# A two-layer decoder trunk on one core: transposing DMAs take a later place on SP's queue, and an unused two-column product goes ahead of the second layer's queries

## The chip, the core and the metric

The kernel runs on one core of one Trainium2 chip. A core has TensorE (PE: products, and PEld: its weight loads), VectorE (DVE), ScalarE (ACT), GpSimd (POOL) and SyncE (SP), each with a queue of its own that is worked off in order, and 16 DMA engines that all queues share. The metric is the time of the whole program on the device in microseconds. Engines wait for each other through semaphores only; an instruction that waits holds back all that stands behind it on its engine.

## What is computed

```python
DEPTH, SEQ, D_MODEL, D_FF = 2, 256, 1024, 2816
def reference(x, norm_mix, norm_ffn, hgrn_w_in, ..., ffn_w13, ffn_w2, final_norm):
    h = x                                          # (1, 256, 1024) float32
    for layer in range(DEPTH):
        y = rms_norm(h, norm_mix[layer])
        if layer % 2 == 0: y = hgrn2_mixer(y, ...)  # gated linear recurrence, 8 heads of 128
        else:              y = moba_mixer(y, ...)   # 8 heads of causal attention with a position bias
        h = h + y
        h = h + swiglu(rms_norm(h, norm_ffn[layer]), ffn_w13[layer], ffn_w2[layer])
    return rms_norm(h, final_norm)
def swiglu(h, w13, w2):
    g, u = jnp.split(h @ w13, 2, axis=-1)
    return (silu(g) * u) @ w2
```

With 256 tokens the second layer's attention is one causal block of 256 keys for each head; its queries, keys and values are `h @ w_in` in three parts of 1024 columns.

## The kernel before

**Products.** Each float32 operand is split into a high part and a rest (`xh`, `xl` of the activations, `whi`, `wlo` of the weights), and three products stand for one: `xh*whi`, `xh*wlo`, `xl*whi`. In most of the work (`mm_w`) a piece of 128 x 128 weights is loaded into TensorE and 256 tokens stream through it (products of 256 columns, out in features by tokens). Where the values, or the outputs of the second feed-forward matrix, are wanted in tokens by features (`mm_x`), 128 tokens are loaded and 512 columns of weights stream.

**Weights.** All weights lie in the order of their use in one tensor, in segments of 1024 columns x 128 rows. SP's queue loads a segment into a `raw` buffer (line 521; spare room in `ii` and `bt` serves as extra ones); ScalarE makes `whi` (line 497), VectorE `wlo` (line 502). Six pairs of `whi` and `wlo` exist, so the splits run at most six segments ahead of TensorE.

**Feed-forward.** Each layer has one. Its second matrix is applied by a scheme with 7 instead of 8 products (`Strassen`): it wants differences (`wdiff`, line 533, VectorE) and sums of weights (`wsum`, line 538, VectorE; another one by an accumulating DMA of GpSimd, line 546, that adds a segment onto a loaded one). The gate and up products are taken from PSUM by ScalarE (`gu`, line 1382) and worked into the hidden activations on VectorE and ScalarE (`sgq`, `uu`, `hx`).

**The residual, turned.** The residual `hT` lies in features by tokens; the feed-forward's results are added in tokens by features. So the residual is turned by DMA beside the first part of each feed-forward, in eight pieces of 128 features: ScalarE copies a piece into `flat` (one buffer; line 1505 in the first layer, 1702 in the second), a transposing DMA on SP's queue turns it into one of two `turns` buffers (lines 1508 and 1705), and ScalarE copies it to its place (lines 1511 and 1707). `Strassen.fold` reads it at the end of the feed-forward (line 1454).

**What sets the order.** Nothing is ordered by hand. TensorE's main products are written in the order of the code. All else goes through a planner (`Order`): `od.op(engine, cost, fn, reads, alloc, due, nbytes, late)` files an operation; while TensorE's clock of the plan moves on, `pump` puts on each engine's queue the filed operation that is due first among those that the plan holds ready. `ready` is the planned end of what an operation reads, and of the last use of the buffers it takes, plus 130 ns; a DMA's planned end is its issue, its bytes at 330 bytes a ns, 1900 ns and `late`. The plan only orders: what waits for what on the chip is set by semaphores. `LATE` is 2200 ns.

**Queries.** In the second layer `token_major` makes the values (512 columns each product, into `psA`), then `feature_major` makes for each head the queries and the keys: 24 products of 256 columns into one bank of PSUM. A bank holds 512 columns, of which these use 256. `Stats.finish` has a short product of two columns of its own, called `settle`, in the first layer (line 768).

Of the kernel before, what the change touches and what calls it, by code (L numbers as in the profile page):

```python
# [16 lines left out]
P = 128  # L17
S = 256
# [138 lines left out]


class Op:
    __slots__ = ("eng", "cost", "fn", "deps", "alloc", "due", "seq", "end", "nbytes", "early", "after", "late")  # L160


class Order:
# [15 lines left out]
        self.wait = {"V": [], "A": [], "G": [], "S": [], "T": []}  # L179
        self.seq = 0  # L180

    def op(self, eng, cost, fn, reads=(), writes=(), alloc=(), due=0.0, nbytes=0, early=None, late=0.0):
        o = Op()
        o.early = self.EARLY if early is None else early
        o.after, o.late = None, late
        o.eng, o.cost, o.fn, o.alloc, o.nbytes = eng, cost, fn, tuple(alloc), nbytes
        o.due, o.end, o.seq = self.tile + due, None, self.seq
        self.seq += 1
        deps = []
        for b in reads:  # L190
            deps += b.writers
        for b in writes:
            deps += b.readers
        o.deps = [d for d in dict.fromkeys(deps)]
        for b in reads:
            b.readers.append(o)
        for b in tuple(writes) + o.alloc:
            b.writers.append(o)
        self.wait[eng].append(o)
        return o  # L200
# [20 lines left out]
    def ready(self, o):  # L221
        if o.after is not None and o.after.end is None:
            return None
        t = 0.0
        for d in o.deps:
            if d.end is None:
                return None
            t = max(t, d.end)
        for b in o.alloc:
            f = self.free_at(b.ring)  # L230
            if f is None:
                return None
            t = max(t, f)
        return t + self.LAT

    def emit(self, o, t):
        start = max(t, self.now if o.eng == "T" else self.clock[o.eng])
# [87 lines left out]
def ca(n, ptr=0):  # L325
    return n / 1.2 + 93 + 93 * ptr
# [11 lines left out]
LATE = 2200.0  # L338
# [3 lines left out]
def hybrid_trunk(ctx: ExitStack, tc: tile.TileContext, wts, xT, par, gfin, tab, masks, out):  # L342
    nc = tc.nc
    V, A, G, T = nc.vector, nc.scalar, nc.gpsimd, nc.tensor
# [5 lines left out]
    od = Order()  # L350
# [57 lines left out]
    def bank(g, held=False):  # L408
        return rings["ps" + g].new(held)

    def main_bank(g):

        b = bank(g, held=True)
        r = b.ring
        od.need(lambda: od.free_at(r))
        b.tile = r.make()
        r.past.append(b)
        return b
# [7 lines left out]
    def wrote(b):  # L426
        b.writers = [Mark(od.now)]
# [8 lines left out]
    segs, c0 = [], 0  # L436
# [4 lines left out]
    quads, c = {}, 0  # L441
# [123 lines left out]
    def piece(name, layer, k, c0, n):  # L565
        assert plan[ws["piece"]] == (name, layer, k, c0, n), (plan[ws["piece"]], (name, layer, k, c0, n))
        ws["piece"] += 1
        return sub_piece("", n)
# [20 lines left out]
    def mm(o, a, b, start=False, stop=False):  # L589
        T.matmul(o, a, b, start=start, stop=stop, skip_group_check=True)  # L590
# [23 lines left out]
    def mm_w(o, w, x, start=False, stop=False):  # L614
        mm(o, w.hi, x.hi, start=start)
        od.main(MM)
        mm(o, w.lo, x.hi)
        od.main(MM)
        mm(o, w.hi, x.lo, stop=stop)
        od.main(MM, 1)  # L620
        od.pump()
# [52 lines left out]
    for k in range(KT):  # L674

        o = od.op("S", 60, lambda k=k: nc.sync.dma_start(hT[:, k:k + 1, :], xT[:, k:k + 1, :]),  # L676
                  writes=hb[k:k + 1], nbytes=131072, due=8 * k - 6)
        if k > 1:
# [12 lines left out]
    o = od.op("S", 60, lambda: nc.sync.dma_start(mk.tile, masks), writes=[mk], nbytes=NMK * P, due=65)  # L691
# [6 lines left out]
          due=100).deps.append(Issued(13))  # L698
# [178 lines left out]
            keep["from"] = None  # L877
            free_subs(ws["sub"])

    def feature_major(name, layer, c0, x, g):  # L880
        b = main_bank(g)
        for k in range(KT):
            mm_w(b[:, :S], piece(name, layer, k, c0, P), x[k], start=(k == 0), stop=(k == KT - 1))
        wrote(b)
        b.held = False
        return b
# [6 lines left out]
    for i in range(4):  # L893
# [6 lines left out]
          reads=[pv, x0[3].l], writes=[lbm], due=50)  # L900
    for i in range(2):
        od.op("V", 80, lambda i=i: V.tensor_tensor(le[:, i], gain(5 + i), lbm.tile, op=OP.subtract), reads=[lbm],
              writes=[le], due=50)
# [5 lines left out]
          writes=[oml], due=60)  # L909
# [251 lines left out]
    for h in range(NH):  # L1161
        c = Core(h)
        xx = xs if h else x0
        c.forget(feature_major("hgrn_w_in", 0, D + P * h, xx, "B"))
        c.query(feature_major("hgrn_w_in", 0, P * h, xx, "B"))
        c.gate(feature_major("hgrn_w_in", 0, 3 * D + P * h, xx, "B"))
        c.result()
        for b in (*c.Q.values(), *c.K.values(), c.even, c.k1, c.kk):
            old.readers += b.readers + b.writers
        if h == 0:  # L1170
            for k in range(KT):
                x0[k].free()
# [68 lines left out]
    class Place:  # L1241


        end = None
# [19 lines left out]
    c = 0  # L1264
# [225 lines left out]
    x2 = {k: X("x", k) for k in range(KT)}  # L1490
# [12 lines left out]
    def flip_h0(k):  # L1503
        a, b, due = flat.new(), rings["turns"].new(), 60 + 24 * k
        od.op("A", ca(2 * S), lambda: A.activation(a.tile.rearrange("p (z t) -> p z t", z=2),
                                                   words(hT[:, k, :]).rearrange("p (t z) -> p z t", z=2), AF.Copy),
              reads=hb[k:k + 1], alloc=[a], due=due)
        od.op("S", 1200, lambda: nc.sync.dma_start(b.tile.rearrange("p (c f) -> p c f", c=4), a.tile, transpose=True),
              reads=[a], alloc=[b], nbytes=131072, due=due, late=LATE)
        for tt in range(2):  # L1510
            od.op("A", ca(S), lambda tt=tt: A.activation(
                words(halves0[tt][:, k * P:k * P + P]).rearrange("p (f z) -> p f z", z=2),
                b.tile.rearrange("p (z a f) -> p a f z", z=2, a=2)[:, tt], AF.Copy), reads=[b], due=due + 12,
                writes=[quadrants[tt, k // 4][0]])

    for k in range(KT):
        flip_h0(k)
    f = Strassen(0, x1, st1, "A", {"A": (1, 5, 4), "B": (6, 3, 7, 2)}, quadrants,
                 {(1, 0): 7, (0, 0): 9, (0, 1): 11, (1, 1): 13})
# [34 lines left out]
    for nh, tt in ((0, 1), (0, 0), (1, 0), (1, 1)):  # L1554
        b = f.final[nh, tt]
# [5 lines left out]
        if (nh, tt) == (0, 0):  # L1561
# [4 lines left out]
            due=0).deps.extend(f.folds[tt, nh])  # L1566
# [107 lines left out]
              reads=[b3, hi], alloc=[lo], due=22)  # L1674

    for h in range(NH):
        qb = feature_major("moba_w_in", 0, P * h, x2, "A")
        kb = feature_major("moba_w_in", 0, D + P * h, x2, "A")
        attend(h, qb, kb)
    for k in range(KT):  # L1680
# [18 lines left out]
    def flip_h(k):  # L1699

        a, b, due = flat.new(), rings["turns"].new(), 60 + 24 * k
        od.op("A", ca(2 * S), lambda: A.activation(a.tile.rearrange("p (z t) -> p z t", z=2),
                                                   words(hT[:, k, :]).rearrange("p (t z) -> p z t", z=2), AF.Copy),
              reads=hb[k:k + 1], alloc=[a], due=due)
        od.op("S", 60, lambda: nc.sync.dma_start(b.tile.rearrange("p (c f) -> p c f", c=4), a.tile, transpose=True),
              reads=[a], alloc=[b], nbytes=131072, due=due)
        o = od.op("A", ca(2 * S), lambda: A.activation(
            words(ht[:, :, k * P:k * P + P]).rearrange("p a (f z) -> p a f z", z=2),
            b.tile.rearrange("p (z a f) -> p a f z", z=2, a=2), AF.Copy), reads=[b], due=due + 12,
            **(dict(writes=[ht]) if k else dict(alloc=[ht])))  # L1710
        if k:
            o.deps.append(ht.writers[0])

    for k in range(KT):
        flip_h(k)
# [4 lines left out]
    class Final:  # L1720
# [38 lines left out]
        def end(self):  # L1759
# [6 lines left out]
            roots.append(od.op("A", 100, lambda: A.activation(a.tile, s[:, e:e + 1], AF.Sqrt, bias=w[:, :1]), reads=[s, w],  # L1766
                               alloc=[a], due=due))
            one = (lambda o, x, y, op: V.tensor_tensor(o, x, y, op=op)) if tt else \
                (lambda o, x, y, op: V.tensor_scalar(o, x, y, None, op0=op))
            od.op("V", 80, lambda: one(w[:, 1:2], s[:, e:e + 1], w[:, :1], OP.add), reads=[s, w], writes=[w], due=due)  # L1770
# [13 lines left out]
            for i, (lo, n) in enumerate(((192, 320), (0, 192), (512, 256), (768, 256)) if tt else ((0, 512), (512, 512))):  # L1784
# [19 lines left out]
                else:  # L1804
# [3 lines left out]
    f = Strassen(1, x3, st3, "B", {"A": (1, 2, 5, 3), "B": (4, 6, 7)}, quadrants,  # L1808
                 {(0, 1): 15, 2: 18, (0, 0): 20, (1, 0): 25, (1, 1): 28}, lambda: od.op(
        "A", ca(D), lambda: A.activation(gf.tile, gf.tile, AF.Copy, scale=2 * float(D) ** 0.5), reads=[bt], writes=[gf],  # L1810
        due=30))
# [4 lines left out]
    for tt in range(2):  # L1816
        fin = Final(tt)
        for i, (nh, o, n) in enumerate(FIN[tt]):
            b = final[nh, tt]
            f.wait_fold(nh, tt)  # L1820
            for k in f.ks:
                p = w[k, nh]
# [46 lines left out]
```

## Time and profile before

| | |
|---|---|
| time, median of 3 runs | 596.44 us (596.27 to 597.47) |
| the profiled execution | 595.67 us; span of its instructions 593.9 us |
| granted TensorE clock | 0.999 |
| busy: TensorE, VectorE, ScalarE, GpSimd | 585.8, 512.9, 444.2, 59.7 us |
| transposing DMAs, first layer (line 1508) | 8, issued 139.5 to 203.8 us |
| transposing DMAs, second layer (line 1705) | 8, issued 413.7 to 457.7 us |
| values of the second layer end, queries begin | 336.96 us |
| SP's issue of one transposing DMA (second layer) | 1.2 us, landing 2.4 to 5.5 us later (median 3.0) |

All times of rows are microseconds from the first instruction. Rows of a timeline give start, length, engine, line, operation, out<-in, and in brackets the idle time of that engine just before, with what ended it. The lengths of TensorE's products overlap (a product of 256 columns is shown as 0.28 us and the next starts some 0.11 us later), so its pace is read from starts. "PEld" waits are waits of its weight loads. Where a row is merged (x51), its second number is the time that all of them take.

### The profile page before, as it was taken

How to read it: one execution, taken by the hardware profiler on the slowest of the kernel's cores; microseconds unless marked ns; L12 is line 12 of the kernel's file. 1: busy time of each engine (PE TensorE's matmuls, PEld its weight loads, DVE VectorE, ACT ScalarE, POOL GpSimd, SP SyncE). 2: the span in 40 equal slices, each digit the busy share in tenths (PEclk: the TensorE clock that was granted, in tenths of full speed). 3: DMA queues.
4: the chain of work that ended last, by engine and by line, in shares of the span. 5: the costliest groups of instructions: out<-in, count | busy, mean ns of one | idle time of the engine just before them, and what ended most of it. 6: DMA issues, size and time to landing. Idle time of an engine off the chain costs nothing.

```text
span 593.9 us, 11985 instructions
## 1 busy us (share of the span) xinstructions
PE 585.8 (99%) x4439; PEld 557.0 (94%) x4439; DVE 512.9 (86%) x939; ACT 444.2 (75%) x868; POOL 59.7 (10%) x111
## 2 busy tenths in 40 slices
PE   9999999999999999999999999999999999999995
PEld 7899999999999999999988899999999999999984
DVE  5899988869897989999999688877798888888996
ACT  6898998957787767667749778976897766666763
POOL 0044131501100000000000000001100000000003
PEclk9999999999999999999999999999999999999999
DMA  8955552557678898877658877767778977877712
GB/s 279 368 165 196 178 171 85 171 178 208 173 228 225 220 249 255 260 241 236 211 196 219 245 253 192 233 162 242 196 200 233 302 243 239 229 231 225 210 35 73
DMA packets 58755, 125.53 MB, mean 211 GB/s; under 512 B 24712, under 2 KB 29704, under 8 KB 58696
## 3 DMA queue, kind: packets, MB, share of 16 engines
q1 hardware_dynamic: 55352, 115.31, 60.4%
q0 software_dynamic: 2384, 8.72, 8.8%
q10 hardware_dynamic: 960, 0.72, 0.4%
q8 instruction: 35, 0.57, 0.4%
q14 instruction: 24, 0.20, 0.1%
HBM read 118.64 MB, written 1.38 MB: 202 GB/s over the span
## 4 chain that ended last, share of the span: by engine, by line
PE 98%; DMA 1%; DVE 0%; ACT 0%; SPq 0%; issue 0%; DVEq 0%; ACTq 0%
PE psB L590 51%; PE psA L590 47%; DMA raw<-in_w_dram 1%; DVE raw L1791 0%; DVE raw L1737 0%; PE psB L1532 0%; PE psA L765 0%; ACT whi L490 0%; SPq L521 0%; SPq L676 0%; DVEq L1865 0%; ACT fa L1766 0%; ACT sq L1740 0%; DVE fw L1774 0%; PE psB L765 0%
## 5 line engine op out<-in xcount | busy, mean ns | idle before, releaser
L502 DVE TENSOR_TENSOR wlo<-raw,whi 128x1024 fp32r<-128x1024 f32 (+2 forms) x187 | 220.5, 1196 | 22.7 <-ACT whi L497 21.0
L497 ACT ACTIVATE whi<-raw 128x1024 fp32r<-128x1024 f32 (+1 forms) x185 | 188.0, 1035 | 20.2 <-PE psB L590 6.0
L590 PE MATMUL psB<-xh,whi 128*128 128x256 f32 x602 | 169.4, 285 | 0.0
L590 PE MATMUL psB<-xh,wlo 128*128 128x256 f32 x602 | 164.6, 277 | 0.0
L590 PE MATMUL psB<-xl,whi 128*128 128x256 f32 x602 | 160.0, 277 | 0.0
L590 PE MATMUL psA<-xh,whi 128*128 128x256 f32 x539 | 147.4, 277 | 0.0
L590 PE MATMUL psA<-xh,wlo 128*128 128x256 f32 x539 | 147.1, 277 | 0.0
L590 PE MATMUL psA<-xl,whi 128*128 128x256 f32 x539 | 142.3, 277 | 0.0
L590 PEld LDWEIGHTS psB<-xh,wlo 128*128 128x128 f32 x602 | 113.3, 188 | 0.6
L590 PEld LDWEIGHTS psB<-xh,whi 128*128 128x128 f32 x602 | 113.3, 188 | 0.5
L590 PEld LDWEIGHTS psB<-xl,whi 128*128 128x128 f32 x602 | 110.1, 188 | 0.0
L590 PEld LDWEIGHTS psA<-xh,wlo 128*128 128x128 f32 x539 | 101.3, 188 | 0.5
L590 PEld LDWEIGHTS psA<-xh,whi 128*128 128x128 f32 x539 | 101.2, 188 | 0.6
L590 PEld LDWEIGHTS psA<-xl,whi 128*128 128x128 f32 x539 | 98.2, 188 | 0.0
L590 PE MATMUL psB<-whi,hx 128*128 128x512 f32 x174 | 60.0, 392 | 0.0
L590 PE MATMUL psA<-whi,hx 128*128 128x512 f32 (+1 forms) x150 | 51.9, 379 | 0.0
L590 PEld LDWEIGHTS psB<-whi,hx 128*128 128x128 f32 x174 | 32.6, 188 | 6.4
L1386 ACT ACTIVATE sgq<-sgq 128x256 f32<-128x256 f32 x44 | 18.1, 414 | 24.1 <-DVE sgq L1384 24.0
L590 PE MATMUL psB<-wlo,hx 128*128 128x512 f32 x87 | 34.2, 393 | 0.0
L590 PEld LDWEIGHTS psA<-whi,hx 128*128 128x128 f32 x150 | 27.7, 188 | 4.3
L546 POOL DMA_DIRECT2D raw<-in_w_dram x13 | 11.3, 872 | 198.3 <-DVE wsum L538 158.9
L590 PE MATMUL psA<-wlo,hx 128*128 128x512 f32 (+1 forms) x75 | 28.6, 381 | 0.0
(263 smaller groups left out, 947.8 us busy)
## 6 DMA issues: line engine op xcount, KB each, us to landing
raw<-in_w_dram SPq DMA_DIRECT2D x176, 512.0 KB, 4.5
bt<-in_w_dram SPq DMA_DIRECT2D x15, 512.0 KB, 4.8
raw<-in_w_dram POOLq DMA_DIRECT2D x13, 512.0 KB, 5.7
ii<-in_w_dram SPq DMA_DIRECT2D x9, 512.0 KB, 4.3
raw<-in_w_dram SPq DMA_DIRECT2D x7, 256.0 KB, 5.6
hT<-in_x_dram SPq DMA_DIRECT2D x8, 128.0 KB, 5.4
bt<-scr SPq DMA_DIRECT2D x32, 32.0 KB, 5.3
bt<-in_w_dram POOLq DMA_DIRECT2D x2, 512.0 KB, 7.1
```

Of the source, the lines that this page charges most:

```text
L497: oa = od.op("A", ca(n), lambda h=h, r=src, o=o, n=n: A.activation(h[:, :n], r[:, o:o + n], AF.Copy), reads=[src], alloc=[h], due=due)
L502: V.tensor_tensor(lo[:, c:c + m], r[:, o + c:o + c + m], h[:, c:c + m].bitcast(FT), op=OP.subtract)
L546: od.op("G", 1000, lambda: nc.gpsimd.dma_start(b.tile, wts[c0 // CHUNK], accum_op=OP.add), writes=[b], nbytes=2 * 524288, due=due + 1)
L590: T.matmul(o, a, b, start=start, stop=stop, skip_group_check=True)
L1386: od.op("A", ca(S), lambda: A.activation(s.tile, s.tile, AF.Silu), reads=[s], writes=[s], due=due)
```

## The change

1. `Order.op` gets a `lag` that is added to the planned readiness of an operation, and the transposing DMAs of both layers get 3000 ns of it: the plan takes one up 3 us later than it holds its input finished.
2. In the second layer they are also given the planned cost and `late` that those of the first have (1200 ns instead of 60, and `LATE`).
3. `feature_major` of the first head's queries starts with a product of 128 x 128 activations with two columns of themselves into two unused columns of its bank. Nothing reads it.

```diff
-    def op(self, eng, cost, fn, reads=(), writes=(), alloc=(), due=0.0, nbytes=0, early=None, late=0.0):
+    def op(self, eng, cost, fn, reads=(), writes=(), alloc=(), due=0.0, nbytes=0, early=None, late=0.0, lag=0.0):
...
-        o.after, o.late = None, late
+        o.after, o.late, o.lag = None, late, lag
...
-        return t + self.LAT
+        return t + self.LAT + o.lag
...
-    def feature_major(name, layer, c0, x, g):
+    def feature_major(name, layer, c0, x, g, settle=False):
         b = main_bank(g)
+        if settle:
+            mm(b[:, S:S + 2], x[0].hi[:, :P], x[0].hi[:, :2], start=True, stop=True)
...
         od.op("S", 1200, lambda: nc.sync.dma_start(b.tile.rearrange("p (c f) -> p c f", c=4), a.tile, transpose=True),
-              reads=[a], alloc=[b], nbytes=131072, due=due, late=LATE)
+              reads=[a], alloc=[b], nbytes=131072, due=due, late=LATE, lag=3000.0)
...
-        qb = feature_major("moba_w_in", 0, P * h, x2, "A")
+        qb = feature_major("moba_w_in", 0, P * h, x2, "A", settle=(h == 0))
...
-        od.op("S", 60, lambda: nc.sync.dma_start(b.tile.rearrange("p (c f) -> p c f", c=4), a.tile, transpose=True),
-              reads=[a], alloc=[b], nbytes=131072, due=due)
+        od.op("S", 1200, lambda: nc.sync.dma_start(b.tile.rearrange("p (c f) -> p c f", c=4), a.tile, transpose=True),
+              reads=[a], alloc=[b], nbytes=131072, due=due, late=LATE, lag=3000.0)
```

The order of instructions differs at these places. First TensorE, between the last of the values and the first of the queries; before:

```order
L590 MATMUL psA<-whi,xh_4443 128x512
L590 MATMUL psA<-wlo,xh_4443 128x512
L590 MATMUL psA<-whi,xl_4452 128x512
L590 MATMUL psA<-xh_4293,whi 128x256
L590 MATMUL psA<-xh_4293,wlo 128x256
L590 MATMUL psA<-xl_4301,whi 128x256
```

and now:

```order
L590 MATMUL psA<-whi,xh_4443 128x512
L590 MATMUL psA<-wlo,xh_4443 128x512
L590 MATMUL psA<-whi,xl_4452 128x512
L590 MATMUL psA<-xh_4293 128x2
L590 MATMUL psA<-xh_4293,whi 128x256
L590 MATMUL psA<-xh_4293,wlo 128x256
L590 MATMUL psA<-xl_4301,whi 128x256
```

TensorE's queue has the one product more, and is otherwise the same from end to end.

SP's queue in the first layer's feed-forward, where the seventh and the eighth transposing DMA stood (`bt<-scr` are small loads of a table); before:

```order
L521 DMA raw_88<-in_w_dram 128x1024
L1508 DMA_TRANSPOSE turns_2147<-flat 128x4x128
L521 DMA raw_91<-in_w_dram 128x1024
L1277 DMA bt<-scr 16x4x128
L521 DMA raw_86<-in_w_dram 128x1024
L521 DMA ii<-in_w_dram 128x1024
L1277 DMA bt<-scr 16x4x128
L521 DMA raw_89<-in_w_dram 128x1024
L1508 DMA_TRANSPOSE turns_2148<-flat 128x4x128
```

and now, with the fifth and the sixth (lines below the first change are two higher):

```order
L521 DMA raw_90<-in_w_dram 128x1024
L1510 DMA_TRANSPOSE turns_2147<-flat 128x4x128
L521 DMA raw_87<-in_w_dram 128x1024
L1279 DMA bt<-scr 16x4x128
L521 DMA raw_88<-in_w_dram 128x1024
L521 DMA raw_91<-in_w_dram 128x1024
L1279 DMA bt<-scr 16x4x128
L521 DMA raw_86<-in_w_dram 128x1024
L521 DMA ii<-in_w_dram 128x1024
L1279 DMA bt<-scr 16x4x128
L1510 DMA_TRANSPOSE turns_2148<-flat 128x4x128
```

The loads keep their order among themselves; the first transpose has as many loads ahead of it in both layers' new places or more, the eighth of the first layer nine more and the eighth of the second 18 more.

VectorE in the same feed-forward, behind the split of a sum of weights; before:

```order
L502 TENSOR_TENSOR wlo<-wsum,whi 128x1024
L502 TENSOR_TENSOR wlo<-raw_90,whi 128x1024
L502 TENSOR_TENSOR wlo<-raw_91,whi 128x1024
L1384 TENSOR_TENSOR sgq<-gu,rrow 128x256
L533 TENSOR_TENSOR wdiff<-raw_86 128x512
L538 TENSOR_TENSOR wsum<-raw_86,ii 128x1024
L1392 TENSOR_TENSOR uu<-gu,sgq 128x256
L502 TENSOR_TENSOR wlo<-wdiff,whi 128x512
```

and now:

```order
L502 TENSOR_TENSOR wlo<-wsum,whi 128x1024
L533 TENSOR_TENSOR wdiff<-raw_86 128x512
L538 TENSOR_TENSOR wsum<-raw_86,ii 128x1024
L502 TENSOR_TENSOR wlo<-raw_90,whi 128x1024
L1386 TENSOR_TENSOR sgq<-gu,rrow 128x256
L502 TENSOR_TENSOR wlo<-raw_91,whi 128x1024
L1394 TENSOR_TENSOR uu<-gu,sgq 128x256
L502 TENSOR_TENSOR wlo<-wdiff,whi 128x512
```

The difference and the sum of the next weights now stand ahead of two splits. ScalarE's copies around the transposes move with them, and small swaps of the same kind stand at some other places of VectorE and ScalarE in both feed-forwards; every engine has the same instructions as before but for the one product.

More of the change, by code (lines that the diff above doesn't have):

```diff
@@ L159 @@
 class Op:
-    __slots__ = ("eng", "cost", "fn", "deps", "alloc", "due", "seq", "end", "nbytes", "early", "after", "late")
+    __slots__ = ("eng", "cost", "fn", "deps", "alloc", "due", "seq", "end", "nbytes", "early", "after", "late", "lag")
 class Order:
```

## The prediction

> **What bounds the kernel now.** I read the page first (busy times, the chain that ended last), then the stretches, then TensorE's own waits, then TensorE's and the queues' rows in time at the two places where the change can touch it.
>
> The page, busy time of each engine and the chain that ended last:
>
> ```profile
> PE 585.8 (99%) x4439; PEld 557.0 (94%) x4439; DVE 512.9 (86%) x939; ACT 444.2 (75%) x868; POOL 59.7 (10%) x111
> ...
> PE 98%; DMA 1%; DVE 0%; ACT 0%; SPq 0%; issue 0%; DVEq 0%; ACTq 0%
> ```
>
> The end of the run is set by TensorE's stream of products almost alone. The stretches say where (columns: stretch, its length, busy of TensorE, of its weight loads, VectorE, ScalarE, GpSimd with counts, granted clock, DMA share, GB/s):
>
> ```profile
> 139.50:336.90 197.40, 197.40 (x1397) 183.26 (x1397) 176.53 (x274) 143.45 (x235) 11.00 (x12) 1.00 0.78 226
> 336.90:347.90 11.00, 11.00 (x94) 10.96 (x94) 8.64 (x14) 7.39 (x11) 0.00 (x0) 1.00 1.02 336
> 347.90:587.00 239.10, 239.09 (x1874) 229.67 (x1872) 206.90 (x374) 176.37 (x303) 12.92 (x15) 1.00 0.69 203
> ```
>
> From 139.5 us on, which is the part of the order that the change rewrites, TensorE is busy in all but 0.01 us, at the full clock. Rows overlap, so a busy TensorE may still be slowed; its waits are therefore looked at on the weight loads, here all of them from 139.5 to 336.9 us (us in total, times, longest):
>
> ```profile
> PEld psB L590 <- DVE wlo L502: 0.2, 1, 0.2
> PEld psA L590 <- DVE wlo L502: 0.2, 1, 0.2
> PEld psA L590 <- DVE xl L706: 0.2, 1, 0.2
> ```
>
> From 336.9 us to the last product there is no such wait. So what an earlier arrival of anything can win behind 139.5 us is at most these 0.6 us, plus whatever makes the products themselves come faster.
>
> **The change, part by part.**
>
> *The two-column product.* It stands between the last product of the values (512 columns) and the first of the queries (256 columns). TensorE's rows at both ends of the stretch it opens, the group of one of its three operand kinds (31 of each), and a piece of the chain right behind it:
>
> ```profile
> 336.73 0.39 PE L590 MATMUL psA<-whi,xl 128*128 128x512 f32 x1
> 336.96 0.28 PE L590 MATMUL psA<-xh,whi 128*128 128x256 f32 x1
> ...
> 347.91 0.38 PE L590 MATMUL psB<-ff,sgf 128*128 128x128 f32 x2
> ...
> L590 PE MATMUL psA<-xl,whi 128*128 128x256 f32 x31 | 8.7, 281 | 0.0
> ...
> 348.65 5.78 PE psA L590 x51
> ```
>
> From 336.96 to 347.91 us 3 x 31 = 93 products start: 10.95 / 93 = 117.7 ns each. Behind the first scores, the same kind of product on the same operands comes every 5.78 / 51 = 113.3 ns. There are two paces, and the stretch of the change runs in the slower one for its whole length, with no engine waited for. If the short product puts TensorE in the faster pace, 4.4 ns are won on each product.
>
> What the short product itself costs is shown by the one that layer 1 has already, at 134.79 us, and its followers:
>
> ```profile
> 134.79 0.25 PE L590 MATMUL psA<-xh 128*128 128x2 f32 x1
> 134.91 0.36 PE L590 MATMUL psB<-xh,whi 128*128 128x256 f32 x1
> 135.11 0.28 PE L590 MATMUL psB<-xh,wlo 128*128 128x256 f32 x1
> 135.22 0.28 PE L590 MATMUL psB<-xl,whi 128*128 128x256 f32 x1
> 135.35 0.28 PE L590 MATMUL psB<-xh,whi 128*128 128x256 f32 x1
> 135.46 0.28 PE L590 MATMUL psB<-xh,wlo 128*128 128x256 f32 x1
> ...
> 53.67 1.77 PE psB L590 x15
> ```
>
> The short product and the four behind it take 135.46 - 134.79 = 0.67 us, where four at the fast pace are 0.45: a cost of 0.22 us. So the stretch becomes 0.67 + 89 x 0.1133 = 10.75 us instead of 10.95: **-0.20 us**. Bounds: if it cost nothing, 93 x 4.4 ns = -0.41; if the slow pace stays, +0.22. The last row above is why the second is possible: right behind products of 128 columns, 15 products at 53.67 us ran at 1.77 / 15 = 118 ns, so an interruption does not always end the slow pace. I take the middle because the only two-column product in the trace was followed by 113 ns.
>
> The Trainium skill (TensorE: Matmul & The Clock Gate, "Wait — 56ns, not 53.3ns?") gives one start-to-start time for a warm stream, N / 2.4 GHz plus about 2.5 ns, and a floor of about 25 ns for the smallest product. By it 256 columns come every 109 ns (an estimate from that page), there is no slow pace to leave, and the short product is pure cost: 0.03 - 0.16 = -0.13 us, 596.3 us by that page. The trace disagrees on the pace, since the same form shows both 117.7 and 113.3 ns, and on the floor, since the product behind the short one starts 0.12 us after it and the next 0.20 later.
>
> *The transposing DMAs of layer 1* (eight, line 1508). Seven of them move back on SP's queue, by one weight load (the first) to nine (the last), and the ScalarE copies that feed and empty them (0.6 and 2 x 0.4 us) move with it. Nothing is added. On SP a moved one delays what stands behind it by its issue, 1.2 us, as before. What it can free is a wait of SP, and one such wait can be followed to TensorE. SP's rows, the sum of its waits at line 1508 behind one ScalarE line, GpSimd's accumulating load and the landing times of all of its kind (min/median/max), then ScalarE, VectorE and TensorE:
>
> ```profile
> 189.67 0.38 SPq L521 DMA_DIRECT2D raw<-in_w_dram  x1
> 195.91 1.20 SPq L1508 DMA_TRANSPOSE turns<-flat  x1
> 197.22 0.52 SPq L521 DMA_DIRECT2D raw<-in_w_dram  x1
> 198.30 0.38 SPq L521 DMA_DIRECT2D raw<-in_w_dram  x1
> ...
> SPq L1508 <- ACT gu L1382: 8.8, 2, 6.4
> ...
> 200.51 0.86 POOL L546 DMA_DIRECT2D raw<-in_w_dram  x1 [16.96 <-DVE wsum L538]
> ...
> DMA to landing us min/median/max: 5.3/5.9/8.8
> ...
> 209.38 1.06 ACT L497 ACTIVATE whi<-raw 128x1024 fp32r<-128x1024 f32 x1 [2.14 <-DMA raw<-in_w_dram]
> ...
> 210.47 1.23 DVE L502 TENSOR_TENSOR wlo<-raw,whi 128x1024 fp32r<-128x1024 f32 x1 [2.48 <-ACT whi L497]
> ...
> 211.48 0.39 PE L590 MATMUL psA<-whi,hx 128*128 128x512 f32 x1
> 211.76 0.51 PE L590 MATMUL psA<-wlo,hx 128*128 128x512 f32 x1
> 212.10 0.40 PE L590 MATMUL psA<-whi,hx 128*128 128x512 f32 x1
> ```
>
> SP stands at the seventh transpose from 190.1 to 195.9 us because ScalarE has not made its input. The loads it held back then start in a burst, the accumulating load joins them at 200.51 and lands at its longest, 8.8 us later; ScalarE waits 2.14 us for it, VectorE 2.48, and TensorE's two products from 211.48 to 212.10 us take 0.28 and 0.34 us where one of 512 columns takes 336.96 - 336.73 = 0.23. That is 0.16 us of delay. In the new order the fifth transpose stands some two loads ahead of this place and the sixth behind it: inputs that are older than the seventh's here, so SP should stand less and the loads come evenly. Bounds: nothing freed, 0; all freed, -0.16. I take **-0.16**, since landing at the median would have brought the data 2.9 us earlier and 0.2 are enough.
>
> *VectorE's order behind it.* The same rewrite puts a difference and a sum (`wdiff`, `wsum`) ahead of one split of weights. VectorE there, and the product that reads the split first:
>
> ```profile
> 222.68 0.42 DVE L1392 TENSOR_TENSOR uu<-gu,sgq 128x256 f32<-128x256 f32 x1 [0.48 <-ACT sgq L1386]
> ...
> 226.56 1.22 DVE L502 TENSOR_TENSOR wlo<-wsum,whi 128x1024 fp32r<-128x1024 f32 x1
> 227.69 2.35 DVE L502 TENSOR_TENSOR wlo<-raw,whi 128x1024 fp32r<-128x1024 f32 x2
> ...
> 230.30 0.69 DVE L533 TENSOR_TENSOR wdiff<-raw 128x512 f32<-128x512 f32 x1
> 230.90 1.22 DVE L538 TENSOR_TENSOR wsum<-raw,ii 128x1024 f32<-128x1024 f32 x1
> ...
> 230.36 0.28 PE L590 MATMUL psA<-xh,wlo 128*128 128x256 f32 x1
> ```
>
> The first of the two splits ends at 227.69 + 1.22 = 228.91 us, 1.45 us ahead of its product. The two operations that now come first take 0.60 + 1.14 us (start to start), 1.74: late by 0.29. That happens if VectorE reaches this place as late as before. Between 210.47 us and here its longest idle time is the 0.48 us of the first row, so the 2.48 us lost above are what mostly set its lateness; with them gone the split is in time. So the two terms exclude each other: 0 here when the first is won (taken), **+0.29** when it is not.
>
> *The transposing DMAs of layer 2* (eight, line 1705), and where their result is first read:
>
> ```profile
> L1705 SPq DMA_TRANSPOSE turns<-flat x8: 1195/1197/1688, 413.7 to 457.7; - x8
> ...
> 574.69 0.75 DVE L1454 SCALAR_TENSOR_TENSOR ii<-psA,ny,ii 128x512 f32<-128x512 f32 x1 [0.32 <-PE psA L590]
> ```
>
> The last one moves back by 18 weight loads on SP's queue. At 2.7 us a load it is issued near 506 us (an estimate: 457.7 + 18 x 2.7, from 24 products of 113.3 ns for each load of 1024 columns), 68 us ahead of its reader. No TensorE wait exists in this part, so nothing is there to win: 0. If the cover went, a ScalarE pass of 0.7 us late in a split would show first.
>
> Sum: -0.20 - 0.16 + 0 + 0 = **-0.36 us**. It is made against the profiled execution, 595.67 us (span 593.9 and 1.77 around it), so 595.3 there. The median of the runs is 596.44, 0.77 above it; the forecast is 596.44 - 0.36 = **596.1 us**.
>
> **The rivals.**
>
> *SP's burst stays.* The transpose that now stands between the loads still meets the accumulating load on the DMA queues. For it: the number of transfers is the same. Then -0.20 and +0.29: 596.5 us.
>
> *The short product doesn't do what it is there for.* TensorE keeps the 117.7 ns: +0.22 - 0.16 = +0.06, 596.5 us. For it speaks the row of 53.67 us, against it that of 134.79. The Trainium skill's single pace (the page named above) would have the same effect.
>
> *The short product costs next to nothing*: -0.41 - 0.16, 595.9 us. Against it: 0.20 us between the products behind the one in layer 1.
>
> *Slower.* VectorE's difference at the second place now stands ahead of a split and waits for its own load; in the old order it had until 230.30 us. If that load lands late, the split behind it is late with it, and TensorE stops. For the whole to reach +1.2 us against the -0.20 of the short product, TensorE must stop for 1.4: the difference then starts at 227.69 + 1.4 - 0.29 = 228.8 us or later, 1.1 us after VectorE gets there. A load that is 2 us late (the worst accumulating load is 2.9 above its median) gives 0.29 + 2.0 - 0.20 = +2.1: 598.5 us. Against it: in the old order the difference ran without any wait.
>
> *Faster by much.* Not from these parts: -0.41 and the whole 0.6 us of waits make 1.0 us, under the 1.2 below.
>
> **How the numbers follow.** A difference of 0.2%, 1.2 us, is about what a measurement of this kernel can tell from none; the three runs alone lie between 596.27 and 597.47. Forecast 0.45; burst stays 0.22; short product without effect 0.15; short product free 0.05: all of these, 0.87, lie within 0.2%. Slower 0.08. Faster 0.05, for something that this trace does not show. The range takes the four middle cases, 595.9 to 596.5, and the scatter of a median of few runs, half a microsecond: 595.4 to 597.0.
>
> **What would show it.** Right: TensorE's products from the query stretch to the first scores at 113.3 ns each (some 10.75 us in all), no wait of weight loads near 211 us, SP at line 1510 with far less waiting than at 1508. Wrong: 117.7 ns behind the short product; a stop of TensorE near 230 us behind line 502; or any wait of TensorE behind 347 us, where there is none now. A time under 595 or over 598 would say that the bound was not TensorE's stream as I read it.

## The result and the profile after

The changed kernel takes 600.04 us (median of 15 runs, 597.13 to 602.37) against 596.44 (15 runs, 594.84 to 599.33): slower by 0.53%, ratio 1.0053 with a 95% interval of 1.0039 to 1.0067, some 3.2 us by the ratio and 3.6 between the medians. The profiled execution took 597.44 us (span 595.7), near the short end of its runs, so it shows less than the usual loss. Busy time of TensorE and the shares of the chain that ended last, on the page after:

```profile
PE 586.9 (99%) x4440; PEld 557.2 (94%) x4440; DVE 513.2 (86%) x939; ACT 444.2 (75%) x868; POOL 60.9 (10%) x111
...
PE 78%; DMA 8%; DVE 6%; ACT 4%; issue 2%; POOL 1%; SPq 1%; DVEq 0%; ACTq 0%
```

TensorE is as busy as before to 0.2%, and yet only 78% of the chain runs through it, where it was 98%: the chain now leaves it for weight loads, their splits and their sums. The waits of weight loads from 190 us on (us in total, times, longest):

```profile
PEld psB L590 <- ACT gu L1384: 1.0, 1, 1.0
PEld psA L590 <- ACT gu L1384: 0.9, 1, 0.9
PEld psB L590 <- DVE wlo L502: 0.6, 1, 0.6
PEld psA L590 <- DVE xl L706: 0.2, 1, 0.2
```

The last one stood in the kernel before as well. The two on `psB` are in the second layer's feed-forward, where the kernel before had none. The place in rows of TensorE, after:

```profile
517.97 0.39 PE L590 MATMUL psB<-whi,hx 128*128 128x512 f32 x1
518.52 0.51 PE L590 MATMUL psB<-wlo,hx 128*128 128x512 f32 x1 [0.16 <-DVE wlo L502]
...
519.56 0.39 PE L590 MATMUL psB<-whi,hx 128*128 128x512 f32 x1
520.49 0.39 PE L590 MATMUL psB<-xh,whi 128*128 128x256 f32 x1 [0.54 <-ACT gu L1384]
```

Two products of 512 columns take 0.55 and 0.93 us where 0.23 is usual: 1.0 us lost, and 0.1 more on the product behind each. Product by product, TensorE is 0.99 us later than in the kernel before at 516.59 us (515.60 there) and 2.25 at 520.71 (518.46 there), and this difference stays to the end. So 1.25 us are lost here and nothing else behind the queries; of the 1 us ahead of it, some 0.4 lies in the first layer's feed-forward, 0.1 at the short product, and some 0.4 in the first 140 us, which the change doesn't touch. What the two products wait for begins at an accumulating load of GpSimd. That load, the split that waits for it and what is queued behind it on ScalarE, after:

```profile
506.12 0.86 POOL L546 DMA_DIRECT2D raw<-in_w_dram  x1 [15.06 <-DVE wsum L538]
...
514.13 1.06 ACT L497 ACTIVATE whi<-raw 128x1024 fp32r<-128x1024 f32 x1 [2.26 <-DMA raw<-in_w_dram]
...
516.86 0.68 ACT L1709 ACTIVATE ii<-turns 128x512 uint16<-128x512 uint16 x1
...
519.34 0.62 ACT L497 ACTIVATE whi<-wdiff 128x512 fp32r<-128x512 f32 x1
519.86 0.58 ACT L1384 ACTIVATE gu<-psB 128x512 f32<-128x512 f32 x1
```

ScalarE stands 2.26 us for the load, and the copy `gu`, which empties the bank that TensorE wants next, comes behind all of it, with a copy out of `turns` (0.68 us) and the split of `wdiff` (0.62 us) among it; before, the copy stood elsewhere and that split behind `gu`. The low part of the same sum of weights on VectorE and the first product that reads it, before (the first fence) and after (the second):

```profile
511.67 1.23 DVE L502 TENSOR_TENSOR wlo<-raw,whi 128x1024 fp32r<-128x1024 f32 x1
...
515.82 0.39 PE L590 MATMUL psB<-wlo,hx 128*128 128x512 f32 x1
```

```profile
515.23 1.23 DVE L502 TENSOR_TENSOR wlo<-raw,whi 128x1024 fp32r<-128x1024 f32 x1 [2.48 <-ACT whi L497]
...
516.82 0.39 PE L590 MATMUL psB<-wlo,hx 128*128 128x512 f32 x1
```

Before, the split was done at 512.90 and read at 515.82: 2.92 us in hand. After, it is done at 516.46 and read at 516.82: 0.36 in hand, and what follows is late. The time in hand shrinks from 47 us earlier on, at the first sum of this stretch: before, its split runs at 465.11 for 1.22 us and is read at 468.59 (2.26 in hand), after at 467.87 and is read at 469.59 (0.50 in hand). The next two sums have 1.8 and 1.6 us in hand (2.8 and 2.9 before), then comes the one above.

What lies in this stretch that did not before is seen on SP's queue (after):

```profile
459.72 2.03 SPq L1707 DMA_TRANSPOSE turns<-flat  x1
...
477.18 1.72 SPq L1707 DMA_TRANSPOSE turns<-flat  x1
...
488.27 1.20 SPq L1707 DMA_TRANSPOSE turns<-flat  x1
...
499.50 0.33 SPq L521 DMA_DIRECT2D raw<-in_w_dram  x1
503.49 1.21 SPq L1707 DMA_TRANSPOSE turns<-flat  x1
504.80 0.52 SPq L521 DMA_DIRECT2D raw<-in_w_dram  x1
505.41 0.38 SPq L521 DMA_DIRECT2D bt<-in_w_dram  x1
```

Four of the eight transposing DMAs of the second layer now lie between 459 and 505 us; before, all were issued by 457.7, while the splits still had some 4 to 12 us in hand. At the last of them SP stands 3.66 us (499.83 to 503.49) for ScalarE's copy, and two weight loads go out only behind it, at 504.80 and 505.41, right ahead of the accumulating load. The landing times of the five accumulating loads from 455 to 525 us, by the buffer they add onto (count, KB, median us from issue to landing), before and then after:

```profile
raw<-in_w_dram POOLq DMA_DIRECT2D x3, 512.0 KB, 5.7
bt<-in_w_dram POOLq DMA_DIRECT2D x2, 512.0 KB, 7.1
```

```profile
raw<-in_w_dram POOLq DMA_DIRECT2D x3, 512.0 KB, 7.9
bt<-in_w_dram POOLq DMA_DIRECT2D x2, 512.0 KB, 6.0
```

Not all of them are slower. The first and the fourth, whose sums lost the most time in hand, took 8.9 and 7.9 us (5.5 and 6.2 before); the other three took 5.7 to 6.9 (5.7 to 7.1 before).

In the first layer one stop went and another came. Near 211 us TensorE no longer waits. Near 238 us it does (ScalarE, then TensorE, after):

```profile
236.94 1.06 ACT L497 ACTIVATE whi<-ii 128x1024 fp32r<-128x1024 f32 x1 [3.69 <-DMA ii<-in_w_dram]
237.91 0.58 ACT L1384 ACTIVATE gu<-psA 128x512 f32<-128x512 f32 x1
...
237.72 0.40 PE L590 MATMUL psA<-whi,hx 128*128 128x512 f32 x1
238.54 0.39 PE L590 MATMUL psA<-xh,whi 128*128 128x256 f32 x1 [0.42 <-ACT gu L1384]
```

ScalarE has nothing to do for 3.69 us, but the split of an accumulated sum stands at the head of its queue and waits for the load; the copy `gu` behind it is held with it for 1.9 us after the last product it reads (236.05 to 237.91). Before, `gu` ran at 235.91 and the split at 238.24.

### The profile page after: what moved, and what is told of

It reads as the page before. It is cut to its first block, busy times and chain, and to the rows that moved or that the text cites. A ratio compares the mean times of both kernels' runs of the same rounds, so it can differ in the third digit from the quotient of the medians.

```text
span 595.7 us, 11994 instructions
## 1 busy us (share of the span) xinstructions
PE 586.9 (99%) x4440; PEld 557.2 (94%) x4440; DVE 513.2 (86%) x939; ACT 444.2 (75%) x868; POOL 60.9 (10%) x111
## 3 DMA queue, kind: packets, MB, share of 16 engines
HBM read 118.64 MB, written 1.38 MB: 201 GB/s over the span
## 4 chain that ended last, share of the span: by engine, by line
PE 78%; DMA 8%; DVE 6%; ACT 4%; issue 2%; POOL 1%; SPq 1%; DVEq 0%; ACTq 0%
PE psA L590 44%; PE psB L590 34%; DMA raw<-in_w_dram 7%; DVE wlo L502 3%; ACT whi L497 2%; DMA bt<-in_w_dram 1%; DVE wsum L538 1%; POOL tot L993 0%; DVE hx L1410 0%; ACT ii L935 0%; SPq L521 0%; ACT xh L923 0%; ACT gu L1384 0%; DVE wdiff L533 0%; POOL qk L1009 0%
## 5 line engine op out<-in xcount | busy, mean ns | idle before, releaser
L590 PEld LDWEIGHTS psB<-xh,whi 128*128 128x128 f32 x602 | 113.3, 188 | 1.5 <-ACT gu L1384 1.0
L590 PEld LDWEIGHTS psB<-xh,wlo 128*128 128x128 f32 x602 | 113.3, 188 | 0.5
```

## Experiments

For each kernel stand its edit, the expectation, and the measurement (median, and its ratio to the kernel before with the 95% interval, where the ratio is not the quotient of the two medians and differs from it by up to 0.2%). The last column of this table is the sum of the waits of weight loads behind 337 us in the kernel's profile.

| kernel | median us | ratio | interval | waits, us |
|---|---|---|---|---|
| before | 596.4 to 597.0 | 1 | | 0 |
| changed | 600.04 | 1.0053 | 1.0039 to 1.0067 | 1.6 |
| e1_settle | 597.20 | 1.0017 | 1.0003 to 1.0030 | 0 |
| e2_layer1 | 596.17 | 1.0005 | 0.9994 to 1.0015 | 0 |
| e3_layer2 | 599.84 | 1.0061 | 1.0049 to 1.0073 | 2.5 |
| e3_again | 600.46 | 1.0055 | 1.0037 to 1.0074 | 2.1 |
| e4_layer2_cost | 598.37 | 1.0033 | 1.0016 to 1.0049 | 2.2 |
| e7_layer2_lag | 597.81 | 1.0027 | 1.0013 to 1.0040 | 0.9 |
| t_first4 | 602.83 | 1.0102 | 1.0081 to 1.0123 | 7.3 |
| p1_plain | 596.95 | 1.0011 | 0.9998 to 1.0025 | 0.8 |
| p2_plain_before | 596.44 | 0.9999 | 0.9981 to 1.0016 | 0 |
| p3_first4_plain | 600.98 | 1.0068 | 1.0046 to 1.0091 | 5.0 |
| p4_plain3 | 600.32 | 1.0062 | 1.0042 to 1.0083 | 3.6 |
| p5_plain2 | 600.09 | 1.0045 | 1.0032 to 1.0059 | 4.3 |
| g_act | 601.74 | 1.0085 | 1.0068 to 1.0103 | 5.7 |
| e5_after_glate1500 | 601.35 | 1.0102 | 1.0072 to 1.0132 | 3.3 |
| e8_layer1_lag2000 | 597.74 | 1.0010 | 0.9996 to 1.0025 | 0 |

Each profile is one execution, so the column only roughly follows the time. But no kernel without such waits is slower by more than 0.17%, and every one with 1.6 us or more of them is slower by 0.33% or more.

### The change in three parts: e1_settle, e2_layer1, e3_layer2

```diff
 e1_settle: before, and
+        if settle:
+            mm(b[:, S:S + 2], x[0].hi[:, :P], x[0].hi[:, :2], start=True, stop=True)
 e2_layer1: before, and in flip_h0
+              ... late=LATE, lag=3000.0)
 e3_layer2: before, and in flip_h
-        od.op("S", 60, ...
+        od.op("S", 1200, ... late=LATE, lag=3000.0)
```

> The kernel before with the two-column product alone; the order on every other engine is that of before. Theory 1 (the loss lies in where the transposing DMAs now stand): 596.3 to 596.6 us, ratio 1.000 within 0.001, and the run of products behind the short one keeps 117 to 119 ns. Rival (the short product costs something that the one profile hides): 598 us or more, with waits of TensorE near 338 us.

> The kernel before with layer 1's transposing DMAs moved alone (lag 3000), layer 2's as before, no short product. ScalarE's weight split whi<-ii then stands ahead of the copy gu<-psA of 237.9 us, as in the changed kernel. Theory 1 (that split waits for the accumulating load and TensorE for the copy behind it): about half of the loss, 597.0 to 598.5 us, with a wait of TensorE for ScalarE's gu near 237 us in the profile. Rival (layer 2 carries all): 596.2 to 596.6 us, no wait near 237 us.

> The kernel before with layer 2's transposing DMAs moved alone (cost 1200, LATE, lag 3000). Theory 1: the other half or more, 597.5 to 599 us, with waits of TensorE at 517 to 520 us, for ScalarE's gu and VectorE's wlo, and the first wait behind an accumulating load that lands near 514 us. Rival (only the stop near 237 us varies from run to run): 596.2 to 597 us.

The second layer's transposes alone lose what the whole change loses (3.6 us, 2.9 to 4.4, from the ratio; again 1.0055 in e3_again). That is more than the 597.5 to 599 us expected of it. The theory that shared the loss between the layers falls: the first layer's move costs and wins nothing that can be measured (though its profile has a stop of 0.3 us near 238 us, so neither theory of e2 came whole). The waits of e3_layer2 behind 337 us:

```profile
PEld psB L590 <- DVE wlo L502: 1.5, 3, 0.8
PEld psB L590 <- ACT gu L1384: 1.0, 1, 1.0
```

The short product alone came out 0.17% slower, 0.7 us in the medians, with an interval that only just leaves out no change; its profile has no wait behind 337 us, so a cost beyond the 0.1 us seen in rows (below) is not explained. Its profiled execution (598.41 us) is longer than that of the kernel before in parts that the edit leaves as they were: by 1.6 us between 5.6 and 45 us and by 0.9 at 213 us.

### How far back: e4_layer2_cost, e7_layer2_lag, t_first4

```diff
 e4: +  od.op("S", 1200, ... late=LATE)
 e7: +  od.op("S", 60, ... lag=3000.0)
 t_first4: +  od.op("S", 1200 if k < 4 else 60, ... late=LATE if k < 4 else 0.0, lag=3000.0 if k < 4 else 0.0)
```

> Layer 2's planned cost 1200 and LATE alone, no lag: 37 weight loads behind the last. Same as for the lag alone: 596.3 to 597.3 us if the loss lies in the places behind 470 us; 599 us or more if the cost and LATE carry it by what they move on VectorE and ScalarE.

> Layer 2's lag of 3000 alone; planned cost 60 and no LATE, as before. On SP's queue the last of the eight then has 36 weight loads behind it, where the kernel before has 42 and the change 24. Theory A or B, by what is exposed: the last of them stands ahead of the stretch near 503 us where the change loses most, so one accumulating load is late by some 3 us, and the 2 us that the splits have in hand there mostly cover it: 596.3 to 597.3 us. Rival (the lag itself, by its first places, is what costs): 599 us or more.

> Layer 2's cost, LATE and lag for the first four pieces alone, the last four as before: the last has 32 weight loads behind it, between the lag alone and the change, and none stands near 503 us. If the place near 503 us (SP waits there 3.7 us for ScalarE's copy, two weight loads and the accumulating load behind it) is the one that stops TensorE: 596.3 to 597.5 us. If the earlier places (460 to 489 us) do it: 598 to 600 us.

With the last transpose issued at 472.6 us (e4) and 471.2 (e7) the loss is 0.33% and 0.27%; with it at 504.3 (e3) 0.61%. But t_first4, with its last at 490.3, is the worst of all. So TensorE can stop without the place near 503 us, and how far back the last one stands does not set the loss. None of the three came within its forecasts: e4 and e7 lie between their two ranges, t_first4 above both. Its waits behind 337 us, and SP at three of its transposes:

```profile
PEld psB L590 <- DVE wlo L502: 5.5, 8, 1.1
PEld psB L590 <- ACT gu L1384: 1.0, 1, 1.0
PEld psB L590 <- ACT whi L497: 0.8, 1, 0.8
```

```profile
471.29 1.20 SPq L1707 DMA_TRANSPOSE turns<-flat  x1
...
477.95 1.30 SPq L1707 DMA_TRANSPOSE turns<-flat  x1
...
490.25 1.20 SPq L1707 DMA_TRANSPOSE turns<-flat  x1
491.54 0.53 SPq L521 DMA_DIRECT2D raw<-in_w_dram  x1
```

SP stands 8.5, 3.4 and 9.6 us ahead of these three, all in the stretch with some 2 to 3 us in hand, and every weight load behind them waits with it. The accumulating loads that go out 3 us behind the first and the third of them, at 474.74 and 493.37 us, took 9.6 and 10.4 us to land, and TensorE stops at their sums (486.77 and 506.23 us); in e4 and e7 the load 3 and 2 us behind the last transpose took 9.2 and 9.3 us, and e4's stop is at its sum.

### Turning or only standing there: p1, p2, p3

```diff
-  nc.sync.dma_start(b.tile.rearrange("p (c f) -> p c f", c=4), a.tile, transpose=True)
+  nc.sync.dma_start(b.tile, a.tile)
```

p1 is e3_layer2 with this, p2 the kernel before, p3 t_first4; in all three layer 2's residual is then not turned. VectorE and ScalarE of p1 have the same instructions in the same order as those of e3_layer2.

> Layer 2's moved transposing DMAs (layer 1 and the queries as before), but the eight DMAs of layer 2 copy their 128 KB straight instead of turning them: same places on every queue, same bytes; the turning of layer 2's residual is left out. Theory A (where they stand: SP waits at them for ScalarE's copy or doesn't, the weight loads then start in bunches, and the accumulating loads and the sums made of them come late): still 599 to 600 us, with waits of TensorE near 517 to 521 us behind wlo and gu. Theory B (the turning itself keeps the DMA engines from the loads, 1 to 2 us each): 596.2 to 597.0 us, no such wait, and the accumulating loads land within 6.5 us.

> The kernel before with layer 2's eight DMAs copying straight instead of turning, at their old places (the turning is left out). If turning costs only where the splits have little in hand, nothing changes here: 596.0 to 596.8 us. If it delays the loads wherever it stands and TensorE pays everywhere: 594 to 595.5 us.

> The kernel with cost, LATE and lag for the first four pieces of layer 2 alone, its eight DMAs copying straight instead of turning (the turning of layer 2's residual is left out); queues and places as in the turning one (602.83 us). Theory B (what costs is the turning itself beside the loads): 596.5 to 598 us, stops of TensorE between 480 and 560 us together under 1.5 us. Theory A' (SP waits at three of these DMAs for 3 to 10 us for ScalarE's copy, and the loads behind are late): 601 us or more, stops as many as with the turning.

At the old places turning is free (p2), which is the cover that the prediction counted on. At the changed places straight copies bring 599.84 back to 596.95, so something of the turning was what the change paid for. The order of VectorE and ScalarE, which is the same, and SP's standing (3.66 us at the last one here too) cost 0.3 us by the two medians and at most 1.5 by the interval. What was expected beside the time did not come: two short waits are left (0.8 us), and the accumulating loads that add onto `raw` still landed in 8.2 us at the median, not within 6.5. At the places of t_first4 straight copies save 1.9 us and leave 4.1: there most of the loss is not the turning. That it is SP's standing fits the rows above but is not shown, since VectorE's and ScalarE's order moved there as well.

### What of the turning: p4_plain3, p5_plain2, e3_again, g_act

```diff
 p4 +  [nc.sync.dma_start(b.tile[i:j], a.tile[i:j]) for i, j in ((0, 48), (48, 88), (88, 128))]
 p5 +  [nc.sync.dma_start(b.tile[i:j], a.tile[i:j]) for i, j in ((0, 64), (64, 128))]
 g_act: as e3_layer2, but
-  od.op("S", 1200, lambda: nc.sync.dma_start(... transpose=True), ...
+  od.op("A", 1200, lambda: nc.scalar.dma_start(... transpose=True), ...
```

> As the straight copies in the change's places of layer 2 (596.95 us), but each copy is issued in three parts (48, 40 and 40 partitions), so that SP spends about as long on the issue as on a turning one (3 x 0.45 against 1.2 us) while the DMA engines move the same 128 KB in rows of 1 KB; the turning is left out. If what costs in the turning one is its time on the DMA engines: 596.5 to 597.5 us. If it is SP's time of issue, behind which the weight loads start later: 599 us or more.

> Layer 2's transposing DMAs moved alone, a second time, on the chip of the three-part copies: 599.4 to 600.2 us by either theory; the two runs side by side give the turning's share without a change of chip.

> Straight copies in the change's places of layer 2, each issued in two parts (64 partitions each), so that SP's issue takes some 1.2 to 1.5 us, as long as a turning one's and not longer as with three parts (2.1 to 2.9 us); the turning is left out. If SP's time of issue is the whole of what the turning costs: 599 to 600.5 us, splits of the sums near 466 and 514 us with under 0.5 us in hand. If it is half of it, the DMA engines' time the other: 597.5 to 598.7 us.

> Layer 2's eight transposing DMAs with cost, LATE and lag as in the change, but issued from ScalarE's queue, behind the copy that feeds them: SP neither waits for that copy nor spends the issue, the DMA engines turn the same bytes in about the same places (40 weight loads later than layer 1's, the last near 500 us). If SP's queue is what costs: 596.3 to 597.5 us, with the accumulating loads near 461 and 510 us landing within 7 us of their issue, unless ScalarE's 1.2 us for each issue holds a gu up (then waits of TensorE for gu, 598 or more). If the turning on the DMA engines costs: 599 us or more, with waits for wlo behind a sum.

SP's issue of the last of the eight, as one straight copy (p1), two (p5) and three (p4):

```profile
506.00 0.47 SPq L1707 DMA_DIRECT2D turns<-flat  x1
```

```profile
502.91 1.11 SPq L1707 DMA_DIRECT2D turns<-flat  x2
```

```profile
503.84 2.12 SPq L1707 DMA_DIRECT2D turns<-flat  x3
```

Two parts give SP about the time that a turning one takes (1.21 us in the same place), turn nothing, and cost about as much (600.09 us against 599.84 and 600.46; 0.45% against 0.61 and 0.55). The time in hand agrees; it is, at the first and at the fourth sum of the stretch (0.05 or 0.06 means that TensorE waits for the split):

| kernel | first sum, us | fourth sum, us |
|---|---|---|
| before | 2.26 | 2.92 |
| e3_layer2, turning | 0.05 | 0.05 |
| e3_again, turning | 0.06 | 0.17 |
| p4, three straight parts | 0.05 | 0.06 |
| p5, two straight parts | 0.06 | 0.16 |
| p1, one straight copy | 1.20 | 1.59 |

So the turning itself is not needed for the loss: 0.5 to 0.6 us more of SP's queue at the last three of the four places in this stretch (p5's 1.32, 1.11 and 1.11 us against p1's 0.78, 0.47 and 0.47) bring it, unless it is that two DMAs are in flight for one, which these runs don't tell apart.

Three things stay open. At the first place p1's issue took longer than p5's (1.96 against 1.38 us), and yet p1 had more in hand behind it. The loss does not grow with the time of issue: p4 spends 2.1 to 2.9 us and loses no more. And p5's profile, its slowest execution (601.47 us), loses 4 us more between 534 and 540 us, behind an accumulating load that was issued at 523.44 and took 9.7 us, where e3 loses nothing.

That SP is the only way is not shown: with the transposes on ScalarE's queue SP is free of them, and the kernel is slower still (601.74). Its waits behind 337 us:

```profile
PEld psB L590 <- DVE wlo L502: 2.9, 3, 1.1
PEld psB L590 <- ACT whi L497: 2.8, 2, 1.8
```

Splits stand in front here too, but ScalarE now spends the issue time itself and its order is another, and the accumulating loads issued at 508.28 and 527.16 us still take 7.3 and 9.4 us. How much of g_act is ScalarE's issue and how much the turning on the DMA engines stays open.

### Two repairs that were none: e5_after_glate1500, e8_layer1_lag2000

```diff
 e5: the changed kernel, and in quad_sums
-              nbytes=2 * 524288, due=due + 1)
+              nbytes=2 * 524288, due=due + 1, late=1500.0)
 e8: e2_layer1 with lag=2000.0
```

> The changed kernel, and the plan counts 1500 ns more for the accumulating loads of GpSimd's queue to land: the split of the loaded sum then stands behind the copy gu<-psA on ScalarE near 237 us, and later on both engines at many places of both MLPs. The transposing DMAs stay within a few rows of their places. Theory 1 (a copy of the gate and up products queued behind a split that waits for a load): 596.0 to 597.5 us, and no wait for gu near 237 us. Rival (the late loads starve TensorE by themselves, whatever the order behind them): 599.5 to 601 us, as the changed kernel, with waits for whi or wlo in place of gu.

> Layer 1's transposing DMAs alone, with a lag of 2000 ns: the copy gu<-psA near 237 us then stands ahead of the split that waits for the accumulating load, as in the kernel before. If the stop near 211 us of the old order (0.3 to 2.1 us in the profiles so far) goes and the one near 237 us doesn't come: 595.3 to 596.0 us, no wait of weight loads between 204 and 245 us. If the two are not what the time hangs on: 596.2 to 596.8 us.

e5 does put `gu` ahead, and the stops at 238 and 518 us go; but the splits are now planned later everywhere, and TensorE stops for them and for `hx` at other places, for 0.7 us at 307 us and, behind 337 us, from 548 us on:

```profile
PEld psB L590 <- DVE wlo L502: 1.9, 3, 1.1
PEld psB L590 <- DVE hx L1410: 0.7, 1, 0.7
PEld psB L590 <- ACT whi L497: 0.7, 1, 0.7
```

So a better order at the two stops did not bring the time back (601.35 us, a little above the rival's range). Since e5 moved the splits everywhere, it doesn't decide whether the order behind a late load or its lateness is at fault near 518 us. e8 has no stop near 238 us but one of 1.1 us ahead of 216.61, again for `gu`. Its 597.74 us lie above both forecasts, and by the ratio can't be told from before.

## Why the prediction was wrong

*The step that failed* is the one on the transposing DMAs of layer 2: "No TensorE wait exists in this part, so nothing is there to win: 0." From nothing to win it went on to nothing to lose. The cover it named was that of the reader, 68 us away. But the DMAs were moved past 18 weight loads on SP's queue, into the stretch where the splits of sums have 2.3 to 2.9 us in hand, and the cover of those loads was not looked up. The estimate of the last one's place, near 506 us, was close (503.49). This term, put at 0, measured +3.6 us (2.9 to 4.4) alone. It had no upper bound; the eight issues of 1.2 us and SP's standing ahead of them were the rows to take one from. What the step named as the first sign, a pass of ScalarE of 0.7 us late in a split, is there (516.86 us), but p1 has it in the same order and loses 0.1%.

*The short product*, -0.20: the rival "without effect" happened. From the short product at 337.83 us two products start by 338.06 and the third at 338.18, and the pace behind is 117.8 ns as before, so it costs 0.35 - 2 x 0.118 = 0.11 us, inside the bound of +0.22:

```profile
337.83 0.17 PE L590 MATMUL psA<-xh 128*128 128x2 f32 x1
337.86 0.36 PE L590 MATMUL psA<-xh,whi 128*128 128x256 f32 x1
338.06 0.28 PE L590 MATMUL psA<-xh,wlo 128*128 128x256 f32 x1
338.18 0.28 PE L590 MATMUL psA<-xl,whi 128*128 128x256 f32 x1
```

And the premise was one execution's: the slow pace there comes and goes (last section).

*The transposing DMAs of layer 1*, -0.16: right in place and in what SP does, too small in size. SP stands 19.6 us in all ahead of the eight, where it stood 39.0. In thirteen profiles with the old order of layer 1 the waits of weight loads from 204 to 218 us are 0.2 to 2.5 us, 1.1 on the mean; in the changed kernel, e2 and e5 they are 0. So the -0.16 was read from an execution in which this stop was short. What was missed is the new stop near 238 us, 0.9 us in the changed kernel and 0.3 in e2, behind ScalarE's order, which the prediction did not read. Together they leave e2 within 0.2% of before.

*VectorE's order near 230 us*, 0: right, TensorE does not wait for VectorE there.

*The sign.* Slower had 0.08, all of it on a difference of VectorE near 228 us that did not come. The sentence under "what would show it", any wait of TensorE behind 347 us, is what came; it had no price.

## What to carry to other kernels

Before work is moved back on a queue, look up not only when its result is read but what each thing it is moved past has in hand: the end of the split and the start of the product that reads it, load by load. Where that is 2 to 3 us, an issue of 1 us in the wrong place can cost time, even on an engine that is never the bound. And an absence of waits says that nothing can be won there by an earlier arrival, not that nothing can be lost.

## What the runs showed of the hardware

The pace of the query products changes from execution to execution under the same order of TensorE. Between 340 and 346 us it is 117.8 ns in six of the seventeen profiles (before, changed, e1, e2, t_first4, e8) and 113.3 ns in eleven; with the short product it is slow in two of three, without it in four of fourteen. The two executions of e3's kernel show both paces elsewhere, 113.6 and 117.5 ns between 20 and 44 us. What sets the pace stays open. The Trainium skill (TensorE: Matmul & The Clock Gate, "Wait — 56ns, not 53.3ns?") gives one start-to-start time for a warm stream, 109 ns here by its formula (an estimate from that page); no profile shows that in this stretch, and both paces stand at a granted clock of 1.00.

The accumulating loads of the second layer's feed-forward took 5.0 to 12.2 us from issue to landing in the seventeen profiles. What makes one slow is not shown by itself: near 490 us one took 8.8 us in e1 and 8.0 in p2, some 30 us behind the last of the eight DMAs. The Trainium skill (DMA: Bandwidth & Descriptors, "Queues, rings and completion order") has each DMA engine take turns between the queues that have work for it, packet by packet; that would make a load of GpSimd's queue slower beside a bunch of SP's, as 7.9 us after against 6.2 before for the load near 505 us, but no run took the bunch away alone.
